# A hybrid decoder trunk: the feed-forward width cut in parts of 4, 6, 6 and 6 tiles where it was 6, 6, 6 and 4

## The chip, the cores and the metric

The kernel runs on one core of a Trainium2 chip. The metric is the device time of one execution in microseconds, the median of several runs. Inside the core, TensorE (PE in the profile) multiplies matrices, VectorE (DVE), ScalarE (ACT) and GpSimd (POOL) work on tiles of 128 partitions, and SyncE (SP) issues the loads and stores. Each engine takes its instructions in order; semaphores make one wait for another.

## The reference

Two layers over 512 tokens of width 1024, in float32. A layer is a mixer (attention heads beside a state-space group, with one input and one output projection) and a feed-forward block:

```python
FFN_HIDDEN = 2816                        # 22 tiles of 128
h = rmsnorm(x, norm_ffn)
x = x + (silu(h @ w_gate) * (h @ w_up)) @ w_down
...
return rmsnorm(x, final_norm)            # after the last layer
```

The lines above are shortened: the change lies in the feed-forward block, and the mixer is told of only where the order of its work comes out differently.

## The kernel before

Activations lie transposed: hT is eight tiles of 128 features by 512 tokens, the residual stream. Every product is made exact enough by three matmuls per tile of 128 rows: weights are split in a rounded part whi (by ACT) and a rest wlo (by DVE), operands likewise in xh and xl, and PE adds xh·whi, xl·whi and xh·wlo in a PSUM tile (acc, hold or tr).

The 22 tiles of the feed-forward width are taken in parts, in the order of the table PARTS. A part has three steps, in layer():

- gate and up for its tiles, taken in pairs (a load is 256 columns of the weight, 1 MB). In the part that comes first, block() makes them: 8 × 3 = 24 matmuls of 512 columns for each tile of gate, and as many for up. This is called plain here. In all other parts seven() makes a pair of tiles at once, in the manner of Strassen: seven products, each of 4 × 3 matmuls of 256 columns, 84 for a pair's gate and 84 for its up. DVE adds the quarters of the weights (wsum), which are split like the rest, and adds up the products (e, m, o).
- the operand for the down product is split: ACT rounds to xh, DVE subtracts to xl (the list hs2).
- the down pass: for each of the eight tiles of hT one block of 3 matmuls per tile of the part, into acc, and DVE adds acc to hT. Its weights come in four loads of two columns of tiles.

seven() wants operands that are split differently; normed() prepares them during the first part (xw, xt and their splits, list X). In the last part of layer 0 the down pass also splits hT for the next layer's projection. In the last part of the last layer, the down product of the last KTOK = 4 tiles is left to finish(), which makes it with the tokens on the partitions, together with the final norm; it loads its weights as two halves of 1 MB (split in dh and dl) and the norm's row as fw. nf in layer() is the number of tiles of that part that still go through a down pass.

Nothing of the order on an engine is written by hand. Each instruction is added to a plan with a due time (at(), clock) and a cost, and a list scheduler sorts all of them, so that a change in one place can alter the order elsewhere. There are two buffers for raw weights (NRAW), three each for whi and wlo (NWH), and three acc, two hold and three tr tiles in PSUM. Loads stand in SP's queue in the order of the plan, and a load waits there until its buffer is free.

In the mixer, the gate step multiplies four tiles xbc by z on POOL, squares them on ACT, sums the squares on POOL (sq), and PE sums over partitions with a product by ones; DVE scales (var), POOL takes the power (rcol), and PE transposes rcol to a row.

Of the kernel before, what the change touches and what calls it, by code (L numbers as in the profile page):

```python
# [41 lines left out]
RES_G = 6  # L42
NEAR_G = 6.0
GATE7 = 1
PARTS = (6, 6, 6, 4)
HH = S // 2
KQ = KD // 2
NCONV = 12
# [312 lines left out]
def hybrid_trunk(  # L361
# [368 lines left out]
    def layer(l, xs, norm):  # L730
# [333 lines left out]
        r0 = 0  # L1064
        for n_, nt in enumerate(PARTS):
            last = n_ + 1 == len(PARTS)
            hs2 = []
# [131 lines left out]
    def finish(l, hs2):  # L1199

        k0 = PARTS[-1] - KTOK
        t_e = clock[0]
# [96 lines left out]
```

## Time and profile before

| | us |
|---|---|
| runs of the kernel (median of 3) | 1298.68 (1298.63 to 1300.33) |
| the profiled execution | 1299.57 |
| its span, first to last instruction | 1297.8 |
| PE busy | 1281.8 |
| DVE busy | 992.2 |
| ACT busy | 677.9 |
| POOL busy | 139.2 |

Times of rows are counted from the span's start. A matmul's duration in a row is longer than the spacing, since matmuls are pipelined; the spacing of two starts tells what one costs in a stream. In layer 0 the plain part lies at 305 to 371 us, the sevens end at 625, and the last down pass ends at 655; layer 1's mixer lies at 660 to 912, its plain part at 946 to 1009, its last sevens end at 1266, and finish() at the end.

### The profile page before, as it was taken

Reading aid. Unit: us, or ns where it says so; the run is one execution under the profiler, and the core shown is the slowest. Engines: PE = TensorE matmul, PEld = TensorE weight load, DVE = VectorE, ACT = ScalarE, POOL = GpSimd, SP = SyncE. Lnnn points to the kernel's source line nnn. Section 1 sums busy time; section 2 is a strip of 40 time slices with the busy share of each in tenths; the row PEclk is TensorE's granted clock in tenths of the full one; section 3 lists DMA queues with packets and bytes.
Section 4 is the critical chain, followed back from the end, with each engine's and each line's share of the span. In section 5 each row is a group of like instructions: output and inputs, shape, how many; then the busy total and the mean of one; then the engine's idle time right before and its main releaser. Section 6 shows DMA issues by size and latency. Waiting matters only on the chain.

```text
span 1297.8 us, 18639 instructions
## 1 busy us (share of the span) xinstructions
PE 1281.8 (99%) x7316; PEld 1077.6 (83%) x7316; DVE 992.2 (76%) x1678; ACT 677.9 (52%) x1070; POOL 139.2 (11%) x109
## 2 busy tenths in 40 slices
PE   9999999999999999999999999999999999999997
PEld 8877776678889989989888777766788899899896
DVE  7987779668667958959879676886786598597694
ACT  8677656556324524424647686465553244254254
POOL 1013454000000000000000234520000000000000
PEclk9999999999999999999999999999999999999999
DMA  7222221123233233242332222111332432332421
GB/s 242 70 65 66 65 66 65 33 66 98 96 116 113 82 114 98 82 135 70 107 98 78 85 65 65 34 65 33 98 98 82 128 110 80 122 98 74 138 98 65
DMA packets 105736, 115.69 MB, mean 89 GB/s; under 512 B 4656, under 2 KB 95024, under 8 KB 105648
## 3 DMA queue, kind: packets, MB, share of 16 engines
q1 hardware_dynamic: 105504, 114.23, 28.1%
q8 instruction: 58, 0.95, 0.3%
q14 instruction: 30, 0.25, 0.1%
q10 hardware_dynamic: 144, 0.26, 0.1%
HBM read 112.39 MB, written 2.10 MB: 88 GB/s over the span
## 4 chain that ended last, share of the span: by engine, by line
PE 89%; DVE 6%; POOL 1%; ACT 1%; issue 1%; DMA 1%; POOLq 0%; ACTq 0%
PE acc L476 68%; PE hold L476 10%; PE tr L476 7%; PE tr L474 3%; DVE wlo L424 2%; DMA raw<-in_w_up_dram 1%; DVE xbc L435 0%; POOL xbc L424 0%; DVE xl L424 0%; DVE hT L424 0%; DVE sa L430 0%; POOL qr L424 0%; ACT whi L461 0%; DVE xl L435 0%; DVE sa L1004 0%
## 5 line engine op out<-in xcount | busy, mean ns | idle before, releaser
L476 PE MATMUL acc<-xh,whi 128*128 128x512 f32 (+1 forms) x1552 | 562.9, 363 | 3.1 <-DVE hT L424 1.8
L476 PE MATMUL acc<-xl,whi 128*128 128x512 f32 (+1 forms) x1552 | 550.8, 355 | 0.2 <-DVE xl L424 0.2
L476 PE MATMUL acc<-xh,wlo 128*128 128x512 f32 (+1 forms) x1536 | 544.6, 355 | 0.0
L461 ACT CAST whi<-raw 128x1024 fp32r<-128x1024 f32 (+3 forms) x248 | 205.4, 830 | 291.6 <-PE acc L476 266.6
L476 PEld LDWEIGHTS acc<-xh,whi 128*128 128x128 f32 x1552 | 293.8, 189 | 54.2 <-issue 11.8
L476 PEld LDWEIGHTS acc<-xh,wlo 128*128 128x128 f32 x1536 | 290.5, 189 | 42.0 <-DVE wlo L424 0.3
L476 PEld LDWEIGHTS acc<-xl,whi 128*128 128x128 f32 x1552 | 293.9, 189 | 37.3 <-issue 0.7
L424 DVE TENSOR_TENSOR wlo<-raw,whi 128x1024 fp32r<-128x1024 f32 (+2 forms) x240 | 237.4, 994 | 17.6 <-ACT whi L461 17.0
L424 DVE TENSOR_TENSOR hT<-hT,acc 128x512 f32<-128x512 f32 x104 | 71.1, 685 | 110.9 <-PE acc L476 110.2
L461 ACT CAST whi<-wsum 128x1024 fp32r<-128x1024 f32 x64 | 67.2, 1050 | 84.4 <-PE tr L476 40.4
L424 DVE TENSOR_TENSOR wlo<-wsum,whi 128x1024 fp32r<-128x1024 f32 x64 | 78.1, 1221 | 14.3 <-ACT whi L461 14.0
L476 PE MATMUL hold<-xh,wlo 128*128 128x256 f32 x256 | 72.6, 283 | 0.3 <-DVE wlo L424 0.3
L476 PE MATMUL hold<-xh,whi 128*128 128x256 f32 x256 | 72.5, 283 | 0.0
L476 PE MATMUL hold<-xl,whi 128*128 128x256 f32 x256 | 72.4, 283 | 0.0
L594 POOL TENSOR_TENSOR rcol<-var,nhalf 128x4 f32<-128x4 f32 x8 | 8.1, 1018 | 563.6 <-DVE var L430 559.0
L463 ACT ACT_TABLE_LOAD x49 | 62.9, 1283 | 5.0 <-DVE xbc L435 3.0
L435 DVE SCALAR_TENSOR_TENSOR xbc<-cu,prm,xbc 128x511 f32<-128x511 f32 (+2 forms) x72 | 58.2, 815 | 0.8
L463 ACT ACTIVATE sa<-sa,mx 128x512 f32<-128x512 f32 (+3 forms) x64 | 36.0, 563 | 26.2 <-DVE mx L1004 26.2
L476 PEld LDWEIGHTS hold<-xh,wlo 128*128 128x128 f32 x256 | 49.1, 192 | 0.5 <-DVE wlo L424 0.5
L476 PEld LDWEIGHTS hold<-xh,whi 128*128 128x128 f32 x256 | 49.1, 192 | 0.5
L476 PEld LDWEIGHTS hold<-xl,whi 128*128 128x128 f32 x256 | 49.1, 192 | 0.5
L424 DVE TENSOR_TENSOR wsum<-raw 128x512 f32<-128x512 f32 x64 | 42.2, 686 | 1.2 <-DMA raw<-in_w_up_dram 0.9
(231 smaller groups left out, 1834.9 us busy)
## 6 DMA issues: line engine op xcount, KB each, us to landing
raw<-in_w_in_dram SPq DMA_DIRECT2D x24, 1024.0 KB, 5.1
raw<-in_w_gate_dram SPq DMA_DIRECT2D x22, 1024.0 KB, 5.2
raw<-in_w_up_dram SPq DMA_DIRECT2D x22, 1024.0 KB, 5.2
raw<-in_w_down_dram SPq DMA_DIRECT2D x24, 768.0 KB, 4.8
raw<-in_w_out_dram SPq DMA_DIRECT2D x8, 1024.0 KB, 5.1
raw<-in_w_out_dram SPq DMA_DIRECT2D x8, 512.0 KB, 6.5
hT<-in_xT_dram SPq DMA_DIRECT2D x8, 256.0 KB, 4.8
raw<-in_w_down_dram SPq DMA_DIRECT2D x4, 512.0 KB, 3.6
```

Of the source, the lines that this page charges most:

```text
L424: lambda: ENG[eng].tensor_tensor(R(o), R(a), R(b), alu))
L435: lambda: nc.vector.scalar_tensor_tensor(R(o), R(a), R(s), R(b), op0, op1))
L461: nc.scalar.copy(R(o), R(a))
L463: nc.scalar.activation(R(o), R(a), func, **kw)
L474: nc.tensor.transpose(R(p[0]), R(p[1]), R(p[2]))
L476: nc.tensor.matmul(R(p[0]), R(p[1]), R(p[2]), start=p[3], stop=p[4])
L594: lambda: nc.gpsimd.tensor_tensor(R(self.r), R(v), R(nhalf), ALU.pow))
```

## The change

The table of parts is put in another order. The part that comes first, and so goes plain, has four tiles, and the three that go by seven products have six each: nine pairs by sevens in a layer where there were eight, and two plain where there were three.

```diff
-PARTS = (6, 6, 6, 4)
+PARTS = (4, 6, 6, 6)
```

In layer() this makes nf = 6 − 4 = 2 in the last part of the last layer, where it was 0: there is now a down pass over two tiles ahead of finish(). In finish() k0 = PARTS[-1] − KTOK is 2. Over the program PE gets 7015 rows where it had 6871, DVE 1691 for 1646, SP 148 for 144.

First place: PE in layer 0, where four tiles are done. Of before, the first gate matmuls of the third plain pair (xh_2690 and the like are the layer's normed input):

```order
L476 MATMUL acc_3228<-xh_2690,whi_3156 128x512
L476 MATMUL acc_3228<-xl_2703,whi_3156 128x512
L476 MATMUL acc_3228<-xh_2690,wlo_3171 128x512
L476 MATMUL acc_3228<-xh_2722,whi_3156 128x512
L476 MATMUL acc_3228<-xl_2747,whi_3156 128x512
```

Of the change, at the same place the down pass of the four tiles: xh_2982, xh_3081, xh_3184 and xh_3287 are the four operands, and the rows between those shown are the first two operands for two more columns (12 rows).

```order
L476 MATMUL acc_3250<-xh_2982,whi_3156 128x512
...
L476 MATMUL acc_3250<-xh_3184,whi_3156 128x512
L476 MATMUL acc_3250<-xl_3194,whi_3156 128x512
L476 MATMUL acc_3250<-xh_3184,wlo_3162 128x512
L476 MATMUL acc_3250<-xh_3287,whi_3156 128x512
L476 MATMUL acc_3250<-xl_3289,whi_3156 128x512
```

The down pass has moved to the place of the third pair, and its last operand is used 21 matmuls after its first.

Second place: SP's queue at the end of layer 1. Of before, the last loads (fw is the final norm's row, the two of 128x4x512 are finish()'s weights):

```order
L480 DMA raw_11439<-in_w_gate_dram 128x8x256
L1207 DMA fw_11465<-in_final_norm_dram 128x512
L1207 DMA fw_11477<-in_final_norm_dram 128x512
L480 DMA raw_11559<-in_w_down_dram 128x4x512
L480 DMA raw_11700<-in_w_down_dram 128x4x512
L480 DMA raw_11744<-in_w_up_dram 128x8x256
```

Of the change:

```order
L480 DMA raw_11729<-in_w_up_dram 128x8x256
L1207 DMA fw_11769<-in_final_norm_dram 128x512
L1207 DMA fw_11780<-in_final_norm_dram 128x512
L480 DMA raw_11866<-in_w_down_dram 128x4x512
L480 DMA raw_12001<-in_w_down_dram 128x4x512
L480 DMA raw_12063<-in_w_down_dram 128x2x256
L480 DMA raw_12134<-in_w_down_dram 128x2x256
L480 DMA raw_12146<-in_w_down_dram 128x2x256
L480 DMA raw_12188<-in_w_down_dram 128x2x256
```

The last up is ahead of finish()'s loads now, and behind them stand the four loads of the new two-tile down pass.

Third place: PE in layer 1's mixer, where the gate step's sum (ones, sq) and its row (rcol) are made among the projection's matmuls (acc) and the state-space group's work (xbc transposes, xdec, hold). Of before:

```order
L474 MATMUL tr_7202<-ident_230,xbc_7150 128x128
L476 MATMUL acc_7160<-xh_6236,whi_7081 128x512
...
L476 MATMUL acc_7160<-xh_6257,wlo_7085 128x512
L476 MATMUL tr_7224<-ones_72,sq_6941 128x1 x4
L476 MATMUL tr_7234<-xdec_7222,btok_6544 128x512
L476 MATMUL hold_7243<-ee_7157,xdt_7219 64x128 x2
L476 MATMUL hold_7246<-ee_7157,xdt_7219 64x128 x2
L474 MATMUL tr_7249<-ident_230,xbc_6977 128x128
...
L474 MATMUL tr_7254<-ident_230,rcol_7238 128x128 x4
```

Of the change, the same instructions:

```order
L476 MATMUL tr_7317<-ones_72,sq_7043 128x1 x4
L474 MATMUL tr_7326<-ident_230,xbc_7089 128x128
...
L476 MATMUL acc_7271<-xh_6338,whi_7185 128x512
...
L476 MATMUL acc_7271<-xh_6360,wlo_7197 128x512
L474 MATMUL tr_7345<-ident_230,rcol_7333 128x128 x4
L476 MATMUL tr_7353<-xdec_7343,btok_6644 128x512
L476 MATMUL hold_7361<-ee_7266,xdt_7341 64x128 x2
L476 MATMUL hold_7364<-ee_7266,xdt_7341 64x128 x2
```

The ones product has moved ahead of the four transposes and the six matmuls of the projection, and the rcol transposes ahead of xdec and hold. On ACT, the last two squares come ahead of the conv step of the next tile there, where the last one came behind it and behind a weight rounding.

## Rows read from the trace of the kernel before

**Rows 1.** The page: busy us (share, instructions) of each engine; the chain's shares.

```profile
PE 1281.8 (99%) x7316; PEld 1077.6 (83%) x7316; DVE 992.2 (76%) x1678; ACT 677.9 (52%) x1070; POOL 139.2 (11%) x109
PE 89%; DVE 6%; POOL 1%; ACT 1%; issue 1%; DMA 1%; POOLq 0%; ACTq 0%
```

**Rows 2.** Waits of PE: in total, times, longest, in us.

```profile
PE tr L476 <- POOL sq L424: 1.0, 1, 1.0
...
PE acc L476 <- DVE xl L424: 0.2, 1, 0.2
```

**Rows 3.** The chain, in order of time: start, us, what.

```profile
308.37 85.71 PE acc L476 x378
...
418.44 5.76 PE acc L476 x48
```

**Rows 4.** One stretch: us, busy us of the engines, clock, DMA share, GB/s.

```profile
396.30:456.60 60.30, 60.30 (x498) 60.04 (x498) 54.37 (x80) 29.87 (x40) 0.00 (x0) 1.00 0.29 93
```

**Rows 5.** Layer 0's last down pass: three pieces of the chain, and PE's timeline.

```profile
627.26 0.63 ACT xh L461
...
627.92 0.70 DVE xl L424
...
626.39 0.39 PE L476 MATMUL acc<-xl,whi 128*128 128x512 f32 x1
...
628.66 0.50 PE L476 MATMUL acc<-xl,whi 128*128 128x512 f32 x1 [0.22 <-DVE xl L424]
```

**Rows 6.** Timeline of DVE and of PE in layer 0's plain part.

```profile
341.08 0.69 DVE L424 TENSOR_TENSOR ga<-acc,rstd 128x512 f32<-128x512 f32 x1 [3.52 <-PE acc L476]
...
346.19 0.69 DVE L424 TENSOR_TENSOR xl<-ga,xh 128x512 fp32r<-128x512 f32 x1 [0.69 <-ACT xh L461]
...
342.24 0.39 PE L476 MATMUL acc<-xh,whi 128*128 128x512 f32 x1
```

**Rows 7.** The chain in layer 1's last sevens.

```profile
1244.55 8.37 DMA raw<-in_w_up_dram
...
1255.42 0.74 PE hold L476 x4
```

**Rows 8.** DMA issues: how many, KB of each, median us to landing.

```profile
raw<-in_w_down_dram SPq DMA_DIRECT2D x4, 512.0 KB, 3.6
...
fw<-in_final_norm_dram SPq DMA_DIRECT2D x2, 256.0 KB, 5.6
```

**Rows 9.** PE's timeline in layer 1's mixer, and a stretch of it.

```profile
768.89 0.60 PE L474 MATMUL tr<-ident,xbc 128*128 128x128 f32 x4
...
771.92 1.05 PE L476 MATMUL tr<-ones,sq 128*128 128x1 f32 x8 [1.03 <-POOL sq L424]
772.83 1.35 PE L476 MATMUL tr<-xdec,btok 128*128 128x512 f32 x2
...
778.33 1.02 PE L476 MATMUL tr<-xdec,btok 128*128 128x512 f32 x2
...
774.00:777.00 3.00, 3.00 (x18) 2.56 (x18) 1.85 (x3) 2.30 (x3) 1.53 (x2) 0.51 0.41 138
```

**Rows 10.** PE's timeline at the same step of layer 0's mixer.

```profile
132.39 0.66 PE L476 MATMUL hold<-ee,xdt 128*64 128x128 f32 x8
132.98 0.50 PE L476 MATMUL acc<-xh,whi 128*128 128x512 f32 x1
...
134.48 0.60 PE L474 MATMUL tr<-ident,rcol 128*128 128x128 f32 x4
134.91 0.60 PE L474 MATMUL tr<-ident,xbc 128*128 128x128 f32 x4
```

**Rows 11.** POOL's timeline in layer 1's mixer.

```profile
765.50 1.74 POOL L424 TENSOR_TENSOR xbc<-xbc,z 128x512 f32<-128x512 f32 x1
770.09 1.77 POOL L424 TENSOR_TENSOR sq<-sq,sq 128x512 f32<-128x512 f32 x1 [2.85 <-ACT sq L463]
```

**Rows 12.** The page's groups: busy, mean ns of one, idle time before.

```profile
L476 PEld LDWEIGHTS hold<-xh,wlo 128*128 128x128 f32 x256 | 49.1, 192 | 0.5 <-DVE wlo L424 0.5
```

## The prediction

> **What bounds the kernel now.** I read the page's engine totals first, then the chain of work that ended last, then who waited for whom, then stretches of the timeline. TensorE (PE) is busy for 1281.8 of 1297.8 us and holds 89% of the chain; VectorE (DVE) is busy 992.2 us and holds 6% [rows 1]. So the time is PE's stream of matmuls plus PE's waits. The list of waits is short, single waits of up to 1.0 us such as the one for a sum of squares on GpSimd (POOL), and 0.2 us for one xl [rows 2]. An edit pays only if it shortens PE's stream or removes one of these waits, and it costs if it makes a new one.
>
> **The swap itself.** A part of the feed-forward width (gate and up products, then the down product) is either plain, 24 matmuls of 512 columns for each tile's gate and the same for its up, or by seven products of 256 columns. One pair of tiles costs 96 matmuls of 512 columns plain, or 2 × 84 = 168 of 256 columns by sevens. Long unbroken pieces of the chain give the spacing: 85.71 us for 378 matmuls of 512 columns, 0.2267 us each, and 5.76 us for 48 of 256 columns, 0.120 us each [rows 3]. A plain pair takes 96 × 0.2267 = 21.76 us, a seven pair 168 × 0.120 = 20.16 us. One pair per layer changes sides: −1.60 us, and **−3.2 us** for two layers. The down product has 22 tiles either way, so its matmuls stay.
>
> The Trainium skill ("TensorE: Matmul & The Clock Gate", section "Back-to-back issue gap") speaks against this change: it gives, for a sustained stream of weight load and matmul pairs, some 81 ns at 128 columns and 131 ns at 512. Between these 256 columns would take about 98 ns (estimate from that page), and 168 × 98 ns against 96 × 131 ns makes the seven pair 3.9 us dearer per layer. The same section's gap for a matmul by itself, N/2.4 + 2.5 ns, gives 20.71 against 18.34 us, which would be −4.7 us in all. The trace sides with neither figure at 512 columns (0.2267 us).
>
> Does DVE keep up? A seven pair also wants sums and splits of weights from DVE. In a stretch of three seven pairs DVE is busy 54.37 of 60.30 us and PE has no gap [rows 4]. Before the change two parts have three pairs and one has two; after it three have three. The extra pair therefore runs as those do, behind a down pass in which DVE gets ahead. I cost it at nothing. If that lead is missing, the first seven of the first such part waits: the order puts the X operands' splits closer to it now. I allow up to 1 us per layer for this in the range.
>
> **Layer 0, the last part.** Its down pass is now six tiles long, not four. In the four-tile pass PE reaches the last pair's operand 12 or 13 matmuls after the last seven, too soon: from 626.39 to 628.66 it makes six steps where 6 × 0.2267 = 1.36 us would do, and the chain there runs over xh and xl to the matmul [rows 5]. That is 0.9 us. In the order of the six-tile passes 18 full matmuls lie between, 4.1 us, and the list of waits has one single wait for such an xl, the one of the four-tile pass [rows 2, 5]. **−0.9 us**, from 0 to −0.9.
>
> **Both layers, the first part.** The short pass doesn't vanish; it moves to the plain part (first place in the order). PE comes to it at 342.24. Its last tile's operand, xh and xl, is wanted 21 and 22 matmuls later, at 347.0 and 347.2. DVE starts the last gate at 341.08, and in before reaches xl at 346.19, finished 346.88 [rows 6]; in the changed order two further splits and an xt stand ahead of it, while before it DVE had idle gaps that they fill. I get 346.4 to 347.1 and a wait of 0.2 us: **+0.4 us** for two layers. Bounds: 0, and 1.0 us each, the nearest row being the stall of the four-tile pass above.
>
> **Layer 1, the tail.** The last part now has six tiles, of which finish() takes four, so a down pass over two tiles appears, with four loads of 256 KB at the end of SP's queue, behind the two finish loads (second place). Before the change the load queued there was the last up: issued 1244.55, landed 8.37 us later, PE restarted at 1255.42 [rows 7], about 0.5 us lost. That wait goes, since this up is now ahead of the finish loads. What comes next: call T the start of the last gate seven. A seven lasts 84 × 0.120 = 10.1 us. The second finish load's last split stands six DVE instructions (0.7 us or less) behind an m that needs 48 matmuls of the up seven, so it ends about T + 16.1 + 3.3 = T + 19.4. Only then has the second small load a buffer. PE wants its weights at T + 20.2 + 3 × 1.36 = T + 24.2. With the 3.6 us that a 512 KB load takes [rows 8] and 1.3 us for rounding and subtraction (xh and xl in [rows 5]) they are there at T + 24.3. I add 0.4 us for a sum that has to leave its PSUM buffer: about +0.5, against −0.5. **0 us**; bounds −0.5 (nothing late) and +2 (a load that takes 5.6 us, as the fw loads do [rows 8]). The eight extra hT additions lie beside PE's matmuls. What follows PE's last matmul is the same work.
>
> **Layer 1's mixer, which the diff doesn't touch.** The planner's list comes out differently here (third place). Before, PE ends a group of six and then idles until 771.92 for the sum of squares; the light work behind it runs on with the granted clock at 0.51 from 774 to 777, its 1.2 GHz level, and the next column resumes at 778.33 [rows 9]. From 768.89 to there are 9.44 us. The same instructions unhindered take about 6.0 us: four transposes 0.36, twelve matmuls at 0.2267 plus a refill after light work 3.0, the ones product 0.91 (771.92 to 772.83), xdec 0.3, hold 0.59, rcol 0.43, transposes 0.36 (layer 0 did the last ones at full clock [rows 10]). So 3.4 us are lost. In the changed order the ones product comes ten matmuls earlier, six full matmuls follow before the rcol transposes, and POOL's last two squares are no longer held by ScalarE's conv step: in before POOL was done with its products at 767.24 and sat until 770.09 [rows 11]. POOL would end near 769.5, PE arrives at 768.9: 0.65 us of waiting, and no long light stretch. That would save 2.8 us; later waits of this mixer hang on DVE and POOL and take some of it back, so I count **−2 us**. Bounds: −3.4 (no loss left) and +2: if the sum comes no earlier than 771.9, PE waits 3.0 us for it, two more than the 1.03 us of the row, and what else was lost stays.
>
> **Sum:** −3.2 − 0.9 + 0.4 + 0 − 2 = −5.7 us. The profiled execution took 1299.57 us, which gives 1293.9; it lay 0.9 above the median of the runs, 1298.68, which gives 1293.0. I predict 1293.4. All bounds at once reach from −8.0 to +4.8 (1 us per layer for DVE's lead among them).
>
> **Rivals.**
> - *The mixer gains nothing* (the wait moves to rcol or further down that mixer). For it: DVE's var still stands behind a weight split that follows the conv step. Sum −3.7: 1294.9 to 1295.9. Chance 0.25.
> - *No change that can be measured.* The swap's 3.2 us are eaten by later waits: 1 us each in the short passes, 1 to 2 us in the tail, 0 to +1 in the mixer: −0.2 to +1.8, 1298.5 to 1300.5, with half of them 1296.5. Against it: the waits have separate causes. Chance 0.11.
> - *Slower: the tail's two-tile pass.* If each 256 KB load took x, the second chunk would be x − 3.2 late and the fourth, whose buffer comes free with the second's splits, x − 5.5 more: 2x − 8.7, or 8.0 us at the 8.37 us of [rows 7]. Without the mixer's gain that makes 1298.7 − 3.7 + 8.0 = 1303.0. It decides from x of about 7.5 us on. Against it: the 8.37 us landed while the finish load was still moving. Chance 0.05.
> - *Weight loads set the pace of sevens.* A 128 × 128 load lasts 192 ns [rows 12]; not overlapped, 168 of them take 32.3 us per pair, and the time would be near 1320. Against it: the spacing of 0.120 us in the same stream [rows 3]. It is what the skill's sustained figures above would mean for the sign; the row decides. Chance 0.01.
> - *More gain than forecast* (mixer at its bound, tail without loss): under 1291. Chance 0.06.
> - The forecast itself, 1291.0 to 1294.9: 0.52.
>
> **From these to the numbers.** 0.2% is 2.6 us, about what a measurement here tells from no change; faster means under 1296.1. The forecast, the larger gain and 0.20 of the first rival lie there: 0.78. The rest of it and the second rival make same, 0.16; slower is 0.06. The range 1290.8 to 1297.4 takes in the forecast, the first rival and the near edge of the second (0.82 or so).
>
> **What would show it.** Right: PE's 512-column matmuls fall by 192 and 256-column ones rise by 336 at the same spacings; layer 0's last down pass has no gap; the first down pass has one of a few tenths; the tail's second chunk stalls under 1 us; the granted clock stays at 1.00 in layer 1's mixer, and the feed-forward of that layer begins 2 us earlier relative to layer 0's end. Wrong: a gap at the first seven behind the plain part, a load behind the finish loads that lands late, or a wait for sq or rcol of over 2 us.

## The result and the profile after

The changed kernel takes 1293.09 us (median of 5 runs, 1292.93 to 1294.29), the kernel before in the same comparison 1300.33 (1298.63 to 1302.46). The ratio is 0.9949, 95% interval 0.9938 to 0.9960: faster by 0.5%. The forecast was 1293.4, a gain of 5.7 us or 0.44% of the time of before.

The page of the changed kernel, engines and chain, answers to [rows 1]:

```profile
PE 1276.5 (99%) x7460; PEld 1080.7 (84%) x7460; DVE 1021.5 (79%) x1730; ACT 689.2 (53%) x1092; POOL 141.3 (11%) x109
PE 92%; DVE 5%; POOL 1%; ACT 1%; issue 1%; DMA 0%; POOLq 0%; DVEq 0%; ACTq 0%
```

PE has 144 instructions more and is busy 5.3 us less: its trace holds 3432 matmuls of 512 columns where it held 3624, and 3024 of 256 columns where it held 2688, as the prediction said. DVE has 29 us more work, and its share of the chain fell. DMA is gone from the chain: before it held 1%, the one load of [rows 7].

**A ruler for all that follows.** Whole spans hide small terms: from the span's start to PE's ones product of layer 0's feed-forward norm, the executions of before and after differ by 1.2 us, over instructions that the change doesn't touch. From that product on, stretches between two fixed instructions can be compared. I use stretch A, from that ones product to the one of layer 1's feed-forward norm (layer 0's feed-forward and layer 1's mixer), and stretch B, from there to the start of PE's last matmul (layer 1's feed-forward). PE's timeline, first of before, then of the changed kernel:

```profile
304.10 0.28 PE L476 MATMUL tr<-ones,sq 128*128 128x1 f32 x2
...
945.07 0.28 PE L476 MATMUL tr<-ones,sq 128*128 128x1 f32 x2
...
1290.18 0.39 PE L476 MATMUL acc<-dl,xh 128*128 128x512 f32 x1
```

```profile
305.31 0.28 PE L476 MATMUL tr<-ones,sq 128*128 128x1 f32 x2
...
941.46 0.28 PE L476 MATMUL tr<-ones,sq 128*128 128x1 f32 x2
...
1284.87 0.39 PE L476 MATMUL acc<-dl,xh 128*128 128x512 f32 x1
```

A is 945.07 − 304.10 = 640.97 before and 636.15 after, −4.8 us; B is 345.11 and 343.41, −1.7 us. Together −6.5 us; the span fell by 5.5, mainly since the changed kernel's profiled execution came 1.2 us later to the ruler's beginning.

**The swap and its spacings**, in the chain of the changed kernel (start, us, what), beside [rows 3]:

```profile
309.57 34.05 PE acc L476 x150
...
367.24 5.76 PE acc L476 x48
...
614.06 38.11 PE acc L476 x168
```

34.05 / 150 = 0.2270 and 5.76 / 48 = 0.120 us: the prices held, in the pair that is new as well. The third row is layer 0's last down pass, now six tiles and the next layer's first products in one unbroken piece; the stall of [rows 5] is gone.

**The first down pass.** PE's timeline has one gap there; DVE's timeline and the chain (the last rows: start, us, what) show what ended before it:

```profile
345.94 0.39 PE L476 MATMUL acc<-xh,wlo 128*128 128x512 f32 x1
346.46 0.47 PE L476 MATMUL acc<-xh,whi 128*128 128x512 f32 x1
```

```profile
344.43 0.68 DVE L424 TENSOR_TENSOR wlo<-raw,whi 128x512 fp32r<-128x512 f32 x1
345.03 0.68 DVE L424 TENSOR_TENSOR xl<-xt,xh 128x512 fp32r<-128x512 f32 x1
345.63 0.68 DVE L424 TENSOR_TENSOR up<-acc,rstd 128x512 f32<-128x512 f32 x1
346.35 0.69 DVE L424 TENSOR_TENSOR ga<-ga,up 128x512 f32<-128x512 f32 x1
347.73 0.69 DVE L424 TENSOR_TENSOR xl<-ga,xh 128x512 fp32r<-128x512 f32 x1 [0.69 <-ACT xh L461]
```

```profile
345.71 0.61 DVE up L424
...
346.46 5.72 PE acc L476 x24
```

The gap is 0.52 − 0.23 = 0.3 us, close to the forecast (0.2), but it isn't where the forecast had it. PE doesn't wait for the last xl, which ends at 348.4, shortly before it is wanted. It stands before the third column of the pass, twelve matmuls in. That column needs a third acc tile, and the last one is still held by up, which DVE reads out only at 345.63, behind three operations of the X operands and two splits of weights. The chain goes from up to that matmul. The splits of weights aren't what it waits for: the later of the two ends at 345.1.

**The tail.** The second small load was issued at 1247.54, and the weights of its first column were split by 1251.98; PE took them at 1252.80 without a gap (SP's queue, DVE and PE in the changed kernel, then how long the small loads took):

```profile
1247.54 0.37 SPq L480 DMA_DIRECT2D raw<-in_w_down_dram  x1
...
1251.56 0.42 DVE L424 TENSOR_TENSOR wlo<-raw,whi 128x256 fp32r<-128x256 f32 x1
...
1252.80 0.39 PE L476 MATMUL acc<-xh,whi 128*128 128x512 f32 x1
...
raw<-in_w_down_dram SPq DMA_DIRECT2D x4, 256.0 KB, 2.7
```

That is 0.8 us to spare. By the prediction's count PE comes to this column at T + 24.24, so T is 1252.80 − 24.24 = 1228.56, and the load was issued at T + 19.0 (T + 19.4 forecast) and landed in 2.7 us (the median of the four), not 3.6. The weights were ready at T + 23.4, where T + 24.3 was forecast.

**Layer 1's mixer**, PE's timeline, one row of DVE's, and the stretches with the granted clock, beside [rows 9]; then one more row of PE's timeline before:

```profile
767.26 1.05 PE L476 MATMUL tr<-ones,sq 128*128 128x1 f32 x8
...
770.72 0.65 PE L474 MATMUL tr<-ident,rcol 128*128 128x128 f32 x4 [0.52 <-POOL rcol L594]
771.20 1.02 PE L476 MATMUL tr<-xdec,btok 128*128 128x512 f32 x2
772.16 0.66 PE L476 MATMUL hold<-ee,xdt 128*64 128x128 f32 x8
...
773.16 0.47 PE L476 MATMUL acc<-xh,whi 128*128 128x512 f32 x1
...
774.72 0.66 PE L476 MATMUL hold<-ee,xdt 128*64 128x128 f32 x8
...
769.41 0.15 DVE L430 TENSOR_SCALAR var<-tr 128x4 f32<-128x4 f32 x1
...
768.00:771.00 3.00, 2.48 (x16) 1.88 (x17) 2.76 (x5) 2.81 (x5) 1.02 (x1) 1.00 0.13 14
771.00:774.00 3.00, 3.00 (x22) 1.94 (x21) 2.99 (x4) 2.98 (x4) 1.54 (x1) 1.00 0.98 333
```

```profile
776.79 0.56 PE L476 MATMUL acc<-xh,whi 128*128 128x512 f32 x1
```

The wait for the sum of squares is gone. In its place stands a wait of 0.52 us for rcol, which DVE's var holds up (it starts at 769.41); the granted clock stays at 1.00, the 2.4 GHz level, where it was 0.51 before.

The instructions that took 9.44 us before [rows 9] take 774.72 − 767.26 = 7.46 us now, 2.0 us less. An estimate from the rows divides this: xdec, hold, the four transposes behind hold and those of rcol took 776.79 − 772.83 = 3.96 us before, most of it at the lower level, and take 773.16 − 770.72 = 2.44 us now. That is 1.5 us for the clock, and the waits, 1.03 us before and 0.52 now, are the rest.

### The profile page after: what moved, and what is told of

Same layout as the page of the kernel before. It is cut to its first block, busy times and chain, and to the rows that moved or that the text cites. A ratio compares the mean times of both kernels' runs of the same rounds, so it can differ in the third digit from the quotient of the medians.

```text
span 1292.3 us, 19046 instructions
## 1 busy us (share of the span) xinstructions
PE 1276.5 (99%) x7460; PEld 1080.7 (84%) x7460; DVE 1021.5 (79%) x1730; ACT 689.2 (53%) x1092; POOL 141.3 (11%) x109
## 4 chain that ended last, share of the span: by engine, by line
PE 92%; DVE 5%; POOL 1%; ACT 1%; issue 1%; DMA 0%; POOLq 0%; DVEq 0%; ACTq 0%
PE acc L476 69%; PE hold L476 12%; PE tr L476 8%; PE tr L474 3%; DVE wlo L424 1%; DVE xl L424 1%; POOL xbc L424 0%; DVE hT L424 0%; DVE sa L430 0%; POOL qr L424 0%; DVE sa L1004 0%; DVE qr L424 0%; DMA w<-in_w_in_dram 0%; DVE ee L424 0%; DVE xl L435 0%
## 5 line engine op out<-in xcount | busy, mean ns | idle before, releaser
L476 PE MATMUL acc<-xh,whi 128*128 128x512 f32 (+1 forms) x1552 | 556.1, 358 | 3.2 <-DVE hT L424 1.8
L476 PE MATMUL acc<-xl,whi 128*128 128x512 f32 (+1 forms) x1552 | 543.9, 350 | 0.0
L476 PE MATMUL acc<-xh,wlo 128*128 128x512 f32 (+1 forms) x1536 | 537.7, 350 | 0.0
L461 ACT CAST whi<-raw 128x1024 fp32r<-128x1024 f32 (+4 forms) x256 | 205.3, 803 | 278.2 <-PE acc L476 235.6
L424 DVE TENSOR_TENSOR wlo<-raw,whi 128x1024 fp32r<-128x1024 f32 (+3 forms) x248 | 236.3, 957 | 16.6 <-ACT whi L461 16.2
L461 ACT CAST whi<-wsum 128x1024 fp32r<-128x1024 f32 x72 | 75.6, 1050 | 100.1 <-PE tr L476 39.0
L424 DVE TENSOR_TENSOR wlo<-wsum,whi 128x1024 fp32r<-128x1024 f32 x72 | 87.9, 1221 | 15.8 <-ACT whi L461 15.5
L476 PE MATMUL hold<-xh,wlo 128*128 128x256 f32 x288 | 81.5, 283 | 0.0
L476 PE MATMUL hold<-xl,whi 128*128 128x256 f32 x288 | 81.5, 283 | 0.0
L476 PE MATMUL hold<-xh,whi 128*128 128x256 f32 x288 | 81.4, 283 | 0.0
```

The lines of the kernel that those rows point to most:

```text
L424: lambda: ENG[eng].tensor_tensor(R(o), R(a), R(b), alu))
L461: nc.scalar.copy(R(o), R(a))
L476: nc.tensor.matmul(R(p[0]), R(p[1]), R(p[2]), start=p[3], stop=p[4])
```

## The experiments

Stretches A and B of every kernel, from the starts of the same instructions as above, and the ratio to the kernel before in its own comparison:

| kernel | A, us | B, us | median, us | ratio [95%] |
|---|---|---|---|---|
| before | 640.97 | 345.11 | 1300.33 | |
| changed | 636.15 | 343.41 | 1293.09 | 0.9949 [0.9938, 0.9960] |
| e1_layer0_only | 636.10 | 344.52 | 1294.60 | 0.9957 [0.9945, 0.9970] |
| e2_layer1_only | 641.02 | 343.54 | 1298.77 | 0.9988 [0.9979, 0.9998] |
| e3_gate_later | 641.65 | 345.66 | 1303.05 | 1.0021 [1.0012, 1.0030] |
| e4_6_4_6_6 | 638.44 | 345.63 | 1298.40 | 0.9987 [0.9978, 0.9996] |
| e5_up_first | 635.71 | 343.05 | 1292.40 | 0.9940 [0.9927, 0.9954] |
| e6_square_first | 641.03 | 345.16 | 1300.42 | 1.0002 [0.9993, 1.0011] |
| e7_2_6_8_6 | 654.44 | 362.91 | 1331.35 | 1.0236 [1.0222, 1.0250] |
| e8_4_6_8_4 | 639.79 | 343.98 | 1297.89 | 0.9973 [0.9963, 0.9983] |
| e9_changed_again | 636.10 | 343.42 | 1294.19 | 0.9952 [0.9940, 0.9965] |
| e10_up_first_again | 635.72 | 343.01 | 1292.43 | 0.9940 [0.9927, 0.9954] |

The changed kernel's stretches came back within 0.05 us in a second execution on another occasion (e9), while medians of one kernel differ by 1 us between comparisons. The stretches carry the small terms, as long as no late load falls in one: B differs by 0.6 us between before and e1, whose layer 1 has the same parts.

**One layer at a time.** The parts become a pair of tables, indexed by the layer (e4, e7 and e8 are made in the same way, with one table for both layers; their diffs are shortened to that table and shown against the kernel before):

```diff
-PARTS = (6, 6, 6, 4)
+PARTS = ((4, 6, 6, 6), (6, 6, 6, 4))      # e1; e2: ((6, 6, 6, 4), (4, 6, 6, 6))
-        for n_, nt in enumerate(PARTS):
-            last = n_ + 1 == len(PARTS)
+        for n_, nt in enumerate(PARTS[l]):
+            last = n_ + 1 == len(PARTS[l])
...
-        k0 = PARTS[-1] - KTOK
+        k0 = PARTS[l][-1] - KTOK
```

> The new order of parts in layer 0 alone; layer 1 keeps 6, 6, 6, 4. The list of instructions in layer 1's mixer comes out as in the changed kernel. Theory A (each step of the prediction stands by itself: swap 1.6 us per layer, the four-tile pass's stall in layer 0, the mixer's order): layer 0 gives 2.3 us and the mixer 2.5, so 4.8 us under before (ratio 0.9963), and layer 1's feed-forward keeps the stall of about 0.5 us in front of its last up. Rival B (the mixer's 2.5 us are not from the order, but chance of one execution): 2.3 us under before, ratio 0.9982.

> The new order of parts in layer 1 alone; layer 1's mixer has the order of before. Theory A: the mixer keeps its wait of 1.2 us for the sum of squares and the stretch at half clock; layer 1's feed-forward gives 1.6 (swap) + 0.5 (stall in front of the last up) - 0.3 (gap in the plain part's down pass) = 1.8 us, ratio 0.9986. Rival B (mixer's gain by chance): may show the mixer without wait here too, 4 us under before.

Theory A holds. e1 has the whole gain of A (−4.87 us) and e2 none (+0.05): layer 0's parts alone decide the order of layer 1's mixer, and the wait for sq is back in e2. B falls by 1.57 in e2, for 1.8 expected. In e1, B fell by 0.6 us although its program there is that of before. The stall in front of the last up was missing, since that load landed sooner: the DMA issues of the two executions, before and e1,

```profile
raw<-in_w_up_dram SPq DMA_DIRECT2D x1, 1024.0 KB, 8.4
```

```profile
raw<-in_w_up_dram SPq DMA_DIRECT2D x1, 1024.0 KB, 7.3
```

So that stall of 0.5 us goes with a load that lands in 7.3 or in 8.4 us behind another one. It was there in the traces of before, e3, e6 and e8, with 8.4 to 8.6 us, and is no fixed price; why the load took longer in them isn't shown.

**The mixer's order without the parts.**

```diff
-        gate(0, tx[1] + 2)
+        gate(0, tx[1] + 2 + (3 if l else 0))
```

> Parts as before (6, 6, 6, 4). Only the due time of the gate step in layer 1's mixer is 3 us later, which puts the last two squares ahead of the conv step on ScalarE, and the ones product where PE does not wait long. Theory A: the mixer alone gives about 2.5 us (2 to 3), ratio 0.998, no half clock in that stretch, with nothing of the parts changed. Rival B: no gain, ratio 1.000, the mixer as long as before.

Neither theory: it is slower, A by 0.7 us. The later due time gave the squares the place on ScalarE that they have in the changed kernel, but PE's order became a third one. The sum came 3 us earlier than in before, counted from layer 1's first norm; PE got there earlier still, waited, and later waited for xdec, at full clock (e3's PE timeline):

```profile
771.06 1.05 PE L476 MATMUL tr<-ones,sq 128*128 128x1 f32 x8 [1.28 <-POOL sq L424]
...
787.23 1.13 PE L476 MATMUL tr<-xdec,btok 128*128 128x512 f32 x2 [1.06 <-DVE xdec L424]
...
786.00:789.00 3.00, 1.94 (x7) 1.17 (x7) 3.00 (x5) 2.15 (x4) 0.88 (x1) 1.00 0.00 0
```

As a test of the order alone it failed, because it made another order. A and B grew by 1.2 us together. The medians of that comparison differ by 2.9 us; the profiled execution also came 2.1 us later to the ruler's beginning than that of before did, and how much of the rest that is, isn't shown.

**The short part in second place.** Parts of 6, 4, 6, 6:

```diff
-PARTS = (6, 6, 6, 4)
+PARTS = (6, 4, 6, 6)
```

> Parts of 6, 4, 6, 6: the plain part has six tiles as before, so no pair changes sides; the short part is second, and the last part has six tiles. Layer 1's mixer has the changed kernel's order. Theory A: no swap, so 3.2 us of the changed kernel's gain are missing. What stays: mixer 2.5, layer 1's last up 0.5, and layer 0's stall of 0.9 us moves to the second part's four-tile down pass and appears in both layers: 2.5 + 0.5 - 0.9 = 2.1 us under before, ratio 0.9984. Rival C (the gain comes from having the short part away from the end, not from the swap): as fast as the changed kernel, ratio 0.995.

Theory A in A: −2.5 us, with no pair swapped and the mixer in the changed kernel's order. The four-tile stall moved with the part: here it stands at 442.66, behind the second part's sevens, in the chain as xh and xl:

```profile
441.98 0.63 ACT xh L461
...
442.63 0.70 DVE xl L424
...
443.38 0.74 PE acc L476 x2
```

It appears in layer 1 too (two gaps of 0.23 and 0.50 and smaller ones), which is why B is 0.5 above before, though e4 has no stall in front of the last up. Rival C, that only the place of the short part counts, falls: 1298.4 is not 1293.

**Up ahead of an X split.** In normed() of the changed kernel both due times are 8 us later:

```diff
-        at(clock[0] - LEAD)
+        at(clock[0] - LEAD + 8)
...
-        at(clock[0] - 8)
+        at(clock[0] - 8 + 8)
```

> The changed kernel with the due times of the X operands' splits 8 us later. The only difference in the order is on VectorE, at the end of the plain part of both layers: the multiplication that writes up (and so frees its PSUM tile) now stands ahead of one X split. Theory D: the gap of 0.30 us in the first down pass (345.94 in the changed kernel's trace) is PE's third column waiting for the PSUM tile that up still holds, so it goes, in both layers: 0.6 us under the changed kernel, and the first seven starts on time. Rival E (the gap is the last pair's operand xl, as the prediction had it): xl comes later or as late, so the gap stays or grows, no gain. Rival F: the X split that was pushed back is late for the first seven, which then waits by up to 0.7 us.

Theory D: the gap is gone in both layers, A and B shrink by 0.44 and 0.36 us. More moved on DVE than was expected: up stands ahead of an xt, two X splits and a split of weights, and the product of ga and up ahead of both X splits; PE's order in the pass is the same. In its repeat (e10) DVE reads up out at 342.83, and PE goes through the place with even steps:

```profile
342.83 0.69 DVE L424 TENSOR_TENSOR up<-acc,rstd 128x512 f32<-128x512 f32 x1
...
345.13 0.39 PE L476 MATMUL acc<-xh,wlo 128*128 128x512 f32 x1
345.36 0.39 PE L476 MATMUL acc<-xh,whi 128*128 128x512 f32 x1
```

The last xl comes earlier too in this version (346.18), but it cannot have been what PE waited for: in the changed kernel PE restarted at 346.46, before that xl was begun, so rival E falls. The first seven isn't late, so rival F falls.

**The last square earlier.** The kernel of before, with one ScalarE instruction one place ahead:

```diff
+                at(ta - (2 if l else 0))
                 nrm.square(xbc[j], E_ADD)
+                at(ta)
```

> The kernel of before, parts 6, 6, 6, 4, where only the squares of the gate step in layer 1's mixer have a due time 2 us earlier. The only difference in the order is on ScalarE: the last square stands ahead of one rounding of weights (1.03 us), still behind the conv step. Theory G (the mixer's loss is the late sum of squares): the sum ends 1.0 us earlier, PE's idle time in front of the ones product falls from 1.03 us to about 0.1, and the mixer from that product to the attention's norm is 1 us shorter, 2 to 2.5 us if the half clock goes with it. Rival H (what counts is how PE's light and dense work alternate, not the sum): PE's order is unchanged, so the half clock stays and the gain is 0 to 0.5 us, other waits taking the rest.

Rival H. The sum was there when PE came, and the gain was nothing (A +0.06). The time went to the next wait, and the clock fell as before (e6: PE's timeline and a stretch; the first row and the last bound the instructions that took 9.44 us before):

```profile
771.05 0.60 PE L474 MATMUL tr<-ident,xbc 128*128 128x128 f32 x4
...
772.89 0.95 PE L476 MATMUL tr<-ones,sq 128*128 128x1 f32 x8
775.03 2.05 PE L476 MATMUL tr<-xdec,btok 128*128 128x512 f32 x2 [1.20 <-DVE xdec L424]
777.01 1.12 PE L476 MATMUL hold<-ee,xdt 128*64 128x128 f32 x8
...
779.07 0.48 PE L476 MATMUL acc<-xh,whi 128*128 128x512 f32 x1
...
780.54 1.02 PE L476 MATMUL tr<-xdec,btok 128*128 128x512 f32 x2
...
774.00:777.00 3.00, 1.97 (x2) 0.50 (x2) 3.00 (x6) 2.97 (x4) 0.76 (x1) 0.67 0.70 212
```

They take 780.54 − 771.05 = 9.49 us here, and from xdec to the end of rcol's transposes 779.07 − 775.03 = 4.04 us, as slow as before. In this order xdec stands right behind the ones product, and DVE isn't ready with it. In the changed kernel six full matmuls and the rcol transposes lie between.

**One more pair by sevens.**

```diff
-PARTS = (6, 6, 6, 4)
+PARTS = (2, 6, 8, 6)
```

> One pair more per layer by sevens: parts of 2, 6, 8, 6, a single plain pair. Everything else as in the changed kernel; the mixer has its order. Theory I (the X operands' splits, some 24 us of VectorE, need the plain part and its down pass as cover): the swap gives another 3.2 us, but plain part and down pass of two tiles last only 32.7 us on PE, against some 45 us of work on VectorE, so the first seven waits about 10 us in each layer: 15 us over the changed kernel, ratio to before about 1.007. Rival J (the sevens take the operands one after another, so little is exposed): 3 us under the changed kernel, ratio 0.9925.

Theory I in sign, and more than twice its size: 38 us slower than the changed kernel. PE's list of waits, the stretch, and DVE in it:

```profile
PE acc L476 <- ACT xh L461: 28.6, 2, 14.3
...
321.00:336.00 15.00, 0.68 (x4) 0.25 (x2) 14.31 (x31) 5.41 (x10) 0.00 (x0) 0.67 0.07 18
...
333.29 0.70 DVE L424 TENSOR_TENSOR up<-acc,rstd 128x512 f32<-128x512 f32 x1
...
335.88 0.69 DVE L424 TENSOR_TENSOR xl<-ga,xh 128x512 fp32r<-128x512 f32 x1 [0.69 <-ACT xh L461]
```

The place was another than expected. PE stops for 14.3 us in each layer in front of the two-tile down pass: the plain pair's own ga and up stand in DVE's queue behind the X operands' splits, so the pass that should have covered these splits can't begin. DVE is busy 14.31 of 15 us there. Smaller waits at the first sevens follow, of 0.8 to 0.9 us.

**The swap with a short last part.**

```diff
-PARTS = (6, 6, 6, 4)
+PARTS = (4, 6, 8, 4)
```

> Parts of 4, 6, 8, 4: the same swap as in the changed kernel, but the last part has four tiles again, the mixer comes out in the order of before, and no two-tile pass exists. Theory A: what is left is the swap, 3.2 us, less two gaps of 0.3 us in the plain part's down pass; the stall of 0.9 us in layer 0's last down pass, the mixer's 2.5 us and the stall in front of layer 1's last up come back: 2.6 us under before, ratio 0.998. Rival K (eight tiles in one part, fewer additions or a better fill): as fast as the changed kernel or faster, ratio 0.995.

A is −1.2 us: one swap (1.6) less the plain part's gap (0.3). The mixer is as long as before, and the stall of [rows 5] is back:

```profile
628.64 0.50 PE L476 MATMUL acc<-xl,whi 128*128 128x512 f32 x1 [0.23 <-DVE xl L424]
```

Rival K falls. Between e8 and the changed kernel A differs by 3.6 us: the four-tile stall and the mixer.

**The two best side by side.**

> The changed kernel once more, beside the version with up first, on the same chip. Expected: about 1293 us, and between the two norm products that bound layer 0's feed-forward 346.7 us, as in its first trace.

> The changed kernel with up ahead of one X split at the end of the plain part, once more, on the same chip as the changed kernel. Theory D: 0.8 us under the changed kernel, 0.4 in each layer, with the gap in the first down pass gone again. Rival: the 0.7 us between their medians were the chip's scatter; both the same.

1292.43 (1292.28 to 1292.71) against 1294.19 (1293.03 to 1294.99): the version with up first beats the changed kernel, as the stretches say, by 0.4 us in each layer; the other 1 us between the medians is not explained by them.

## Why the prediction was right, and where not

- **The swap, −3.2 us: right.** The prices of [rows 3] held, e8 shows one swap in A by itself (1.2 + 0.3 = 1.5 us), and e4 shows what is left without it. The Trainium skill's figures for a sustained stream ("TensorE: Matmul & The Clock Gate", section "Back-to-back issue gap") would have made the sevens dearer; the spacings after the change, 0.2270 and 0.120 us, don't agree with them, and the measurement decides.
- **DVE keeps up at no cost: right here, with its limit shown.** The three stretches of three pairs run without a gap. The condition that the prediction named, the X operands' splits close to the first seven, bites in e7, though mainly on the plain part's own operands and less on the sevens.
- **Layer 0's last part, −0.9 us: right.** The stall follows a four-tile pass behind sevens: in before and e8 at the end, in e4 in second place, not in the changed kernel.
- **The first part, +0.4 us: near in size (a gap of 0.3 each; e5 got back 0.44 and 0.36), wrong in its cause.** The step that failed is "its last tile's operand, xh and xl, is wanted 21 and 22 matmuls later". PE stood earlier, for a PSUM tile that up still held. I had followed the operands of the moved pass and not the tiles that it writes. The chain runs from up to the matmul that stood, and e5, in which DVE reads up out sooner, removes the gap.
- **The tail, 0 us: it came out at about −0.5.** The mechanism was right to 0.4 us (the load's issue); the term was mis-sized by two prices, 3.6 us for a load that took 2.7, and 0.4 us for a PSUM tile that PE didn't wait for. The 0.5 us are the stall of before, and that before ran with it is in part luck, since in e1 a layer 1 of the same parts ran without it.
- **Layer 1's mixer, −2 us: it gave 2.5 (e4's A; e1's A less layer 0), but the reason given fails in part.** The prediction took the late sum of squares as what the stretch lost. e6 brings the sum in time and gains nothing; e3 brings it 3 us earlier and loses. What goes with the gain is PE's order: dense matmuls stand between the ones product and rcol and xdec, so that DVE's and POOL's steps run beneath them. This is read from the rows and not shown by a run that moves those matmuls alone: e3 has dense matmuls behind its ones product too and kept the clock, yet it waited for 1.28 and 1.06 us and was slower. The wait for rcol (0.52 us) that the first rival named did appear. The sum was mis-sized in two places: xdec, priced at 0.3 us unhindered, takes 772.16 − 771.20 = 0.96, so that the instructions there saved 2.0 us and not 2.8; and what the forecast took off for later waits of the mixer didn't come, another 0.5 us were gained outside of them. Of the 2.5 us about 1.5 is the clock, by the estimate above. Which of the several moved instructions would do it alone stays open.
- **The sum.** −5.7 forecast; −6.5 in A and B. Of the difference 0.5 is the tail and 0.5 the mixer, less 0.2 for the plain part's gaps. That the measured time lies within 0.3 us of 1293.4 is in part luck: the kernel before took 1300.33 us in this comparison and not the 1298.68 of the forecast, and the gain between the medians was 7.2 us.

## What to carry to other kernels

When work is moved on the engine that bounds the kernel, ask of the place where it lands for two things: when its operands are ready, and who still holds the tiles that it writes. A product that costs the bounding engine less and a neighbour more pays as long as the neighbour has a stretch of other work to get ahead in; the next step of the same change can take that stretch away, and then it costs more than ten times what it gives (in e7 another 3.2 us for the swap, against some 40 us that waits and what came behind them took). A wait that is removed alone may only uncover the one behind it, so price the whole stretch up to the next dense run and not the wait.

## What was not expected of the hardware

The time from the span's start to the ones product of layer 0's first norm was 28.1 us in one execution (before) and 30.2 in another (e9), over instructions that were the same. From there to the ruler's beginning it was 275.9 to 276.1 us in most executions and 276.6 to 276.8 in three (changed, e4 and e8), though e9 is the changed kernel again. The stretches A and B repeated within 0.1 us (changed and e9, e5 and e10). A 1 MB load behind another one on the same queue landed in 7.3 us in one execution, where PE had no such stall, and in 8.4 to 8.6 in four others, where PE stood for about half a microsecond.
